# Three expert tiles by unsplit float32 products and five by gathers, and projection weights in 4 KB rows

## The chip, the core and the metric

The kernel runs on one core of a Trainium2 chip. A core has TensorE (PE, matrix products; its weight loads are PEld), VectorE (DVE), ScalarE (ACT), GpSimd (POOL, here the issuer of indirect DMAs) and SyncE (SP, here the issuer of the plain DMAs), and 16 DMA engines that all queues share. The metric is device time in microseconds, the median of several runs.

## The reference, cut to what matters

One decoder layer on 1024 tokens of 1024 channels, in float32. A combined projection feeds two groups of heads (stick-breaking attention and a gated linear recurrence), an output projection adds them to the stream, and then comes a layer of single-neuron experts:

```python
q = einsum('td,dhk->thk', xc, w_query)            # 8 heads, two halves of 128
s = einsum('thpk,hpnk->thpn', q, sub_keys)        # 128 keys for each half
top_s, top_i = top_k(s, 16)                       # 16 best of each half
best_s, best_pos = top_k(all 16 x 16 sums, 16)    # 16 best pairs of each head
idx = ...                                         # one of 128 * 128 experts
g = softmax(best_s)
u, v = expert_u[idx], expert_v[idx]               # 8 heads x 16 = 128 experts a token
act = gelu(einsum('td,thkd->thk', xc, u))
y = einsum('thk,thkd->td', g * act, v)
```

So each token takes 128 of 16384 experts, and an expert is one row of 1024 float32 in each of two tables of 64 MB.

## The kernel before

The 1024 tokens are 8 tiles of 128, worked on in five groups (tile 0; 1 and 2; 3 and 4; 5 and 6; tile 7). The stages of the groups (`norm_in`, `in_proj`, `rg_proj`, `rg_lru`, `attention`, `out_proj`, `queries`, `select`) are put out in the order of the string `ORDER`; the framework then lays each engine's instructions into one fixed sequence by a timeline that it simulates when the program is built, and what comes earlier in the program goes first where two could run. Each engine works off its sequence in order.

The experts are computed in two ways.

*Gathered tiles* (0, 1, 2 and 7): `gather_block` takes slots of 128 tokens x 1 expert. For a slot, GpSimd gathers 128 rows of table u (0.524 MB, line 652), VectorE multiplies them with the normalised tokens and sums (line 663), ScalarE and VectorE make the weight, GpSimd gathers 128 rows of v, and VectorE adds them, weighted, to y (line 678). A tile has 128 slots, so 256 gathers. The first `FREE` blocks of 8 slots have no condition; each later block, of one slot, has a ScalarE copy ahead (line 660) that reads a mark which the dense experts write, so that it does not start before its turn. The buffers are `UV` = 4 in the pool `gat` and, once the dense stage has begun, `UV2` more in `gat2`; slots go to the pools by turns.

*Dense tiles* (3, 4, 5 and 6): `gates` builds, for each tile, a matrix of gate weights over all 16384 experts and stores it in DRAM (`gd`, by a product `pg` for each token, line 623). `dense_experts` then goes over 128 blocks of 128 experts. For each, SP loads the block of the transposed u table (`ur`) and of the v table (`vr`), 0.524 MB each, and every fourth time a piece of the gate matrices (`gt`). Operands are split into two parts of type float32r, a high part by ScalarE and the remainder by VectorE (`split`, lines 182 and 183), and each product is three matmuls (`mm`, line 177): the scores `s` (8 chunks of channels x 3, 512 tokens wide), and the outputs, for four tiles and two halves of the channels. Six of these eight outputs stay in PSUM (`acc`); the other two go through a rotating bank (`rot`) every four blocks and are added in SBUF (`yr`).

The projection weights are read as tiles of 128 columns, from the matrix as it stands, so a row of a tile is 512 bytes in DRAM (`columns`, line 188); w_out is read in rows of 2 KB (line 426). Over the five groups these are 100 loads of w_in, 80 of w_q and 40 of w_out, each of 0.524 MB.

Of the kernel before, what the change touches and what calls it, by code (L numbers as in the profile page):

```python
# [7 lines left out]
F32 = mybir.dt.float32  # L8
F32R = mybir.dt.float32r
# [22 lines left out]
UV2 = 3  # L32
TB = 32
GE = 4
# [13 lines left out]
ORDER = "n0 i0 p0 a0 r0 o0 q001 q023 n1 i1 q047 s001 s047 p1 r1 a1 n2 p2 i2 o1 q1 r2 s023 n3 p3 i3 a2 r3 o2 q2 n4 s1 s2 i4 a3 p4 r4 o3 free g3 a4 q3 o4 s3 q4 g4 g5 g6 s4"  # L48
# [9 lines left out]
def layer(ctx, tc, x, w_in, w_out, w_q, vecs, rga, rgx, skT, eu, ev, euT, out,  # L58
          groups=((0,), (1, 2), (3, 4), (5, 6), (7,)), dense=(3, 4, 5, 6), dbg=None):
# [13 lines left out]
    # the banks that the last stages do not use are apart: the dense experts start in them  # L73
# [8 lines left out]
    # gate matrices of the dense tokens: gd[j, block of TB tokens, i, token], for expert i * 128 + j  # L82
# [36 lines left out]
    # means over 512 channels, over the channels of a head  # L119
# [6 lines left out]
    # heads 2 c and 2 c + 1 of 8 to chunk c of channels  # L126
# [14 lines left out]
    # rank16[k, s] = k  # L141
# [6 lines left out]
    # softplus(-lam) = max(-lam, 0) + ln(1 + exp(-|lam|))  # L148
# [18 lines left out]
    def cut(parts_, k, sl=slice(None)):  # L167
        return tuple(t[:, k, sl] for t in parts_)

    def mm(dst, a, b, first=True, last=True):  # L170
        """dst += sum over k of a[k].T @ b[k]: float32, or pairs of float32r parts"""
        n = len(a)
        terms = ((0, 0),) if len(a[0]) == 1 else ((1, 0), (0, 1), (0, 0))
        i = 0
        for u, v in terms:
            for k in range(n):
                nc.tensor.matmul(dst, a[k][u], b[k][v], start=first and i == 0, stop=last and i == len(terms) * n - 1)  # L177
                i += 1

    def split(hi, lo, src):  # L180
        """src as two float32r parts"""
        nc.scalar.activation(hi, src, AF.Copy)  # L182
        nc.vector.tensor_tensor(lo, src, hi.bitcast(F32), op=OP.subtract)  # L183

    def columns(pool, tag, w, c0, name, bufs):
# [37 lines left out]
    # sums of pairs in rows of 8: what no pair takes stays out of reach  # L223
# [3 lines left out]
    # the sums and the normalised rows of the gathered tiles  # L227
# [3 lines left out]
    def norm_in(g):  # L231
# [7 lines left out]
        # x -> h^T  # L239
# [5 lines left out]
    def in_proj(g):  # L245
# [6 lines left out]
        # q, k, v; q stays without its rstd, which the scores take  # L252
        rqk = keep.tile([P, 3, n, 8], F32, tag="rq", name="rq", bufs=2)
        G[g]["rq"] = rqk[:, 1:3]
        for dst, c1, gain, nm in ((kT[:, :, t0:t0 + T], 4, 1, "pk"), (qT, 0, 0, "pq")):
            for c in range(4):
                raw = columns(pj, "wraw", w_in, (c1 + c) * P, "wi", WI)
# [22 lines left out]
        for c in range(4):  # L280
            raw = columns(pj, "wraw", w_in, 1024 + c * P, "wi", WI)
# [6 lines left out]
    def rg_proj(g):  # L288
        """channels on partitions"""
# [4 lines left out]
        for e in range(4):  # L294
            wx = columns(pj, "wraw", w_in, 1536 + e * P, "wx", WI)
# [547 lines left out]
```

## Time and profile before

| | us |
|---|---|
| median of 3 runs | 2895.28 |
| lowest, highest | 2887.94, 2907.56 |
| span of the profiled execution, first to last instruction | 2904.6 |
| TensorE matmul busy | 2659.0 (92%) |
| VectorE busy | 2404.2 (83%) |
| GpSimd busy | 1401.6 (48%) |
| ScalarE busy | 1336.3 (46%) |
| 16 DMA engines, mean | 306 GB/s, 888.90 MB |

The span is the only time that the page has of the profiled execution itself. An engine's busy time is an average over stages with different limits, so the stages are looked at one by one: the projections and heads until about 1490 us, with gathers running beside them, and from there the dense experts, with paced gathers beside them.

### The profile page before, as it was taken

The numbers are of one execution on the slowest core, as the hardware profiler recorded it, in microseconds if no ns is written. First come the engines' busy times: TensorE is split into PE (matmuls) and PEld (weight loads), VectorE is DVE, ScalarE is ACT, GpSimd is POOL, SyncE is SP. The second block draws the span as 40 slices with busy tenths as digits, with TensorE's granted clock in tenths as the row PEclk, the third lists the DMA queues.
The fourth block names the chain that finished last, engine by engine and source line by source line (L and its number), as shares of the span: only waits on it lengthen the run. The fifth ranks groups of instructions, "written<-read, shape, count | busy, mean of one in ns | idle before, by whom it ended". The sixth has DMA issues, their size and how long they took to land.

```text
span 2904.6 us, 38604 instructions
## 1 busy us (share of the span) xinstructions
PE 2659.0 (92%) x12664; PEld 2103.5 (72%) x12664; DVE 2404.2 (83%) x5235; ACT 1336.3 (46%) x3255; POOL 1401.6 (48%) x1110
## 2 busy tenths in 40 slices
PE   7896989888997988988789999999999999999994
PEld 7685757766784576666567888888888888888883
DVE  2168779987998879998879979888888889888898
ACT  4426434434355633986834443434444434444432
POOL 0134654354444443323446546555655556555565
PEclk9997999898997889978889999999999999999997
DMA  8596888899977688987999989999999999999998
GB/s 235 162 325 223 289 308 297 268 308 297 293 237 250 226 288 291 327 285 268 334 321 360 347 315 365 328 338 352 323 347 339 333 325 352 334 348 329 335 331 307
DMA packets 470168, 888.90 MB, mean 306 GB/s; under 512 B 27600, under 2 KB 286672, under 8 KB 467920
## 3 DMA queue, kind: packets, MB, share of 16 engines
q0 software_dynamic: 147456, 536.94, 52.2%
q1 hardware_dynamic: 322512, 349.51, 36.1%
q8 instruction: 100, 1.64, 0.2%
q14 instruction: 100, 0.82, 0.1%
HBM read 841.25 MB, written 45.09 MB: 305 GB/s over the span
## 4 chain that ended last, share of the span: by engine, by line
PE 61%; DMA 13%; DVE 11%; issue 6%; ACT 5%; POOL 3%; SPq 0%; POOLq 0%; DVEq 0%; ACTq 0%
PE s L177 23%; PE acc L177 16%; PE rot L177 5%; DMA v<-in_ev_dram,idx 4%; DMA u<-in_eu_dram,idx 3%; DMA wq<-in_w_q_dram 3%; PE pqq L194 2%; PE pg L623 2%; DVE u L663 2%; PE pxg L194 2%; DVE y L678 2%; PE pv L285 2%; PE po L429 1%; PE z L377 1%; POOL v L652 1%
## 5 line engine op out<-in xcount | busy, mean ns | idle before, releaser
L652 POOL DMA_INDIRECT u<-in_eu_dram,idx x512 | 666.7, 1302 | 702.0 <-DVE y L678 340.5
L652 POOL DMA_INDIRECT v<-in_ev_dram,idx x512 | 665.2, 1299 | 609.7 <-DVE y L678 193.0
L678 DVE SCALAR_TENSOR_TENSOR y<-v,dots,y 128x1024 f32<-128x1024 f32 x512 | 654.9, 1279 | 48.4 <-DMA v<-in_ev_dram,idx 43.4
L663 DVE SCALAR_TENSOR_TENSOR u<-u,h 128x1024 f32<-128x1024 f32 x512 | 617.3, 1218 | 63.3 <-DMA u<-in_eu_dram,idx 62.0
L177 PE MATMUL s<-h2T,uh 128*128 128x512 f32 x2048 | 505.2, 396 | 0.0
L177 PEld LDWEIGHTS s<-h2T,uh 128*128 128x128 f32 x2048 | 385.5, 188 | 93.4 <-issue 0.2
L177 PE MATMUL acc<-vh,wl 128*128 128x512 f32 x768 | 300.1, 391 | 21.3 <-DVE wl L183 21.2
L177 PE MATMUL acc<-vl,wh 128*128 128x512 f32 x768 | 300.5, 391 | 0.1
L177 PE MATMUL acc<-vh,wh 128*128 128x512 f32 x768 | 299.9, 391 | 0.0
L177 PE MATMUL s<-h2T,ul 128*128 128x512 f32 x1024 | 264.3, 398 | 2.0 <-DVE ul L183 2.0
L194 PE MATMUL pqq<-act,wq 128*128 128x256 f32 (+1 forms) x1280 | 243.1, 347 | 10.9 <-DMA wq<-in_w_q_dram 10.9
L194 PEld LDWEIGHTS pqq<-act,wq 128*128 128x128 f32 x1280 | 208.7, 196 | 36.1 <-DMA wq<-in_w_q_dram 13.1
L177 PEld LDWEIGHTS s<-h2T,ul 128*128 128x128 f32 x1024 | 193.2, 189 | 49.3 <-DVE ul L183 1.8
L182 ACT ACTIVATE vh<-vr 128x512 fp32r<-128x512 f32 x256 | 159.1, 627 | 149.1 <-PE acc L177 70.1
L183 DVE TENSOR_TENSOR vl<-vr,vh 128x512 fp32r<-128x512 f32 x256 | 174.4, 687 | 50.6 <-ACT vh L182 47.1
L623 PE MATMUL pg<-oa,ob 128*128 128x128 f32 x1024 | 166.1, 315 | 37.8 <-DVE ob L620 26.6
L623 PEld LDWEIGHTS pg<-oa,ob 128*128 128x128 f32 x1024 | 148.2, 221 | 64.4 <-issue 22.4
L177 PEld LDWEIGHTS acc<-vh,wl 128*128 128x128 f32 x768 | 144.8, 189 | 53.6 <-issue 21.0
L717 ACT ACTIVATE ga<-s 128x512 f32<-128x512 f32 x128 | 76.4, 597 | 222.9 <-PE s L177 221.3
L624 ACT ACTIVATE gs<-pg 128x512 f32<-128x512 f32 x128 | 136.2, 1080 | 86.2 <-PE pg L623 69.4
L183 DVE TENSOR_TENSOR ul<-ur,uh 128x1024 fp32r<-128x1024 f32 x128 | 156.4, 1222 | 14.3 <-ACT uh L182 13.5
L177 PEld LDWEIGHTS acc<-vl,wh 128*128 128x128 f32 x768 | 144.9, 189 | 31.8 <-DVE vl L183 0.5
(238 smaller groups left out, 4445.1 us busy)
## 6 DMA issues: line engine op xcount, KB each, us to landing
vr<-in_ev_dram SPq DMA_DIRECT2D x128, 512.0 KB
ur<-in_euT_dram SPq DMA_DIRECT2D x128, 512.0 KB
wq<-in_w_q_dram SPq DMA_DIRECT2D x80, 512.0 KB
gd<-gs SPq DMA_DIRECT2D x16, 2048.0 KB
gt<-gd SPq DMA_DIRECT2D x32, 1024.0 KB
wi<-in_w_in_dram SPq DMA_DIRECT2D x60, 512.0 KB
wo<-in_w_out_dram SPq DMA_DIRECT2D x40, 512.0 KB
wx<-in_w_in_dram SPq DMA_DIRECT2D x20, 512.0 KB
```

Source lines behind the costliest of these rows:

```text
L177: nc.tensor.matmul(dst, a[k][u], b[k][v], start=first and i == 0, stop=last and i == len(terms) * n - 1)
L182: nc.scalar.activation(hi, src, AF.Copy)
L183: nc.vector.tensor_tensor(lo, src, hi.bitcast(F32), op=OP.subtract)
L194: nc.tensor.matmul(dst, w[:, k, :], act[:, k, :], start=k == 0, stop=k == DK - 1)
L285: nc.tensor.matmul(pv[:, i * P:(i + 1) * P], act[:, k, i * P:(i + 1) * P], raw[:, k, :], start=k == 0, stop=k == DK - 1)
L377: nc.tensor.matmul(zz, qT[pp, h // 2, qs], kT[pp, h // 2, c0:c0 + w], start=True, stop=not diag)
L623: nc.tensor.matmul(pg[:, t * P:(t + 1) * P], ob[:, t, :], oa[:, t, :], start=True, stop=True)
L624: nc.scalar.activation(gs[:, :, t4:t4 + 4].rearrange("p i t -> p t i"), pg.rearrange("p (t i) -> p t i", t=4), AF.Copy)
L652: nc.gpsimd.indirect_dma_start(out=t, out_offset=None, in_=table, in_offset=bass.IndirectOffsetOnAxis(ap=idx[:, s:s + 1], axis=0))
L663: nc.vector.scalar_tensor_tensor(u, u, 1.0, h2, op0=OP.mult, op1=OP.mult, accum_out=dots[:, s:s + 1])
L678: nc.vector.scalar_tensor_tensor(y, v, dots[:, s:s + 1], y, op0=OP.mult, op1=OP.add)
L717: nc.scalar.activation(ga, sp[:, :ND], AF.Gelu_apprx_tanh)
```

## The change

Tile 6 moves from the dense experts to the gathered ones: three tiles (384 tokens) are dense, five gathered. The dense products are no longer split: a matmul of float32 operands takes the place of three of float32r ones, and all six outputs (three tiles, two halves) stay in PSUM, so that `split`, `mm`, the rotating bank and the sums in SBUF go. The first 37 blocks of gathers (296 slots) have no condition (27 before, 216 slots). The pool of gathers in the dense stage has 12 buffers in place of 3, `ur` 4 in place of 3, `vr` 4 in place of 2, and a piece of the gate matrices covers 8 blocks of experts in place of 4, so its rows are 1 KB in place of 512 bytes. w_in, w_q and w_out are laid out on the host so that each partition's share of a tile is one row of 4 KB; the keys `skT` are laid out by head. The gates of tile 6 (`g6`) leave `ORDER`. Comments go.

```diff
-UV2 = 3
+UV2 = 12
-GE = 4
+GE = 8
-FREE = 27
-V0 = 2
-V1 = 5
-UR = 3
-VR = 2
+FREE = 37
+UR = 4
+VR = 4
-ORDER = "... g3 a4 q3 o4 s3 q4 g4 g5 g6 s4"
+ORDER = "... g3 a4 q3 o4 s3 q4 g4 g5 s4"
...
-          groups=((0,), (1, 2), (3, 4), (5, 6), (7,)), dense=(3, 4, 5, 6), dbg=None):
+          groups=((0,), (1, 2), (3, 4), (5, 6), (7,)), dense=(3, 4, 5), dbg=None):
...
-        nc.sync.dma_start(raw, w[:, c0:c0 + P].rearrange("(k p) n -> p k n", p=P))
+        nc.sync.dma_start(raw, w[c])
...
-                nc.sync.dma_start(raw, w_out[q * 256:(q + 1) * 256, c * 512:(c + 1) * 512].rearrange("(k p) n -> p k n", p=P))
+                nc.sync.dma_start(raw, w_out[c, q])
...
-            nc.sync.dma_start(skh, skT[:, 2 * h:2 * h + 2, :])
+            nc.sync.dma_start(skh, skT[h])
...
     def dense_experts():
-        act = [d1.tile([P, DK, ND], F32R, name=f"h2T{i}") for i in range(2)]
+        h2T = d1.tile([P, DK, ND], F32, name="h2T")
         for t, tl in enumerate(dense):
-            r = d1.tile([P, DK, P], F32, tag="ur", name="h2r", bufs=UR)
-            nc.sync.dma_start(r, h2Td[tl])
-            split(*(a[:, :, t * P:(t + 1) * P] for a in act), r)
...
-        quads = [(t, d) for d in range(2) for t in range(nt)]
-        held, rot = quads[:6], quads[6:]
+            nc.sync.dma_start(h2T[:, :, t * P:(t + 1) * P], h2Td[tl])
+        quads = [(t, d) for t in range(nt) for d in range(2)]
+        acc = {q: pd.tile([P, 512], F32, name=f"acc{q[0]}_{q[1]}") for q in quads}
...
         def front(e):
             ur = d1.tile([P, DK, P], F32, tag="ur", name="ur", bufs=UR)
             nc.sync.dma_start(ur, euT[e])
-            uh = d0.tile([P, DK, P], F32R, tag="uh", name="uh", bufs=2)
-            ul = d0.tile([P, DK, P], F32R, tag="ul", name="ul", bufs=2)
-            split(uh, ul, ur)
-            vr = d0.tile([P, D], F32, tag="vr", name="vr", bufs=VR)
-            nc.sync.dma_start(vr, ev[e * P:(e + 1) * P, :])
+            vs[e] = d0.tile([P, D], F32, tag="vr", name="vr", bufs=VR)
+            nc.sync.dma_start(vs[e], ev[e * P:(e + 1) * P, :])
             sp = pd0.tile([P, 512], F32, tag="s", name="s", bufs=2)
-            mm(sp[:, :ND], [cut((uh, ul), k) for k in range(DK)], hk)
-            ga = d1.tile([P, ND], F32, tag="ga", name="ga", bufs=2)
+            for k in range(DK):
+                nc.tensor.matmul(sp[:, :ND], ur[:, k, :], h2T[:, k, :], start=k == 0, stop=k == DK - 1)
+            ga = d1.tile([P, ND], F32, tag="ga", name="ga", bufs=3)
             nc.scalar.activation(ga, sp[:, :ND], AF.Gelu_apprx_tanh)
             gb = ga.rearrange("p (b t) -> p b t", t=TB)
             nc.vector.tensor_tensor(gb, gb, gts[0][:, :, e % GE, :], op=OP.mult)
-            wh = dp.tile([P, ND], F32R, tag="wh", name="wh", bufs=GE + 1)
-            wl = dp.tile([P, ND], F32R, tag="wl", name="wl", bufs=GE + 1)
-            split(wh, wl, ga)
-            wts[e] = (wh, wl)
+            wts[e] = ga
...
         def back(e):
-            for q in held:
-                vprod(acc[q], e, q, e == 0, e == P - 1)
-            if e % GE == GE - 1:
-                for q in rot:
-                    pr = pd0.tile([P, 512], F32, tag="s", name="rot", bufs=2)
-                    for f in range(e - GE + 1, e + 1):
-                        vprod(pr, f, q, f == e - GE + 1, f == e)
...
+            for t, d in quads:
+                nc.tensor.matmul(acc[t, d], wts[e][:, t * P:(t + 1) * P], vs[e][:, d * 512:(d + 1) * 512], start=e == 0, stop=e == P - 1)
...
+    def columns(w):
+        return w.reshape(DK, P, -1, P).transpose(2, 1, 0, 3)
...
+        "x": a["x"][0], "w_in": columns(a["w_in"][0]), "w_q": columns(a["peer_w_query"][0].reshape(D, 2048)),
+        "w_out": a["w_out"][0].reshape(4, 2, P, 2, 512).transpose(3, 0, 2, 1, 4),
```

## Rows read from the trace of the kernel before

**Rows 1.** The page: busy engines; DMA queues (packets, MB, share of time).
```profile
PE 2659.0 (92%) x12664; PEld 2103.5 (72%) x12664; DVE 2404.2 (83%) x5235; ACT 1336.3 (46%) x3255; POOL 1401.6 (48%) x1110
...
q0 software_dynamic: 147456, 536.94, 52.2%
q1 hardware_dynamic: 322512, 349.51, 36.1%
```

**Rows 2.** Windows by stage; engines busy (instructions), clock, DMA share, GB/s.
```profile
0.00:250.00 250.00, 195.12 (x1242) 172.29 (x1242) 100.13 (x413) 109.08 (x264) 49.56 (x59) 0.91 0.76 234
250.00:600.00 350.00, 318.13 (x1533) 245.10 (x1534) 304.46 (x844) 150.95 (x354) 175.48 (x150) 0.92 0.86 288
600.00:1000.00 400.00, 357.95 (x1795) 265.12 (x1794) 348.48 (x942) 196.69 (x436) 189.85 (x158) 0.88 0.82 266
1000.00:1490.00 490.00, 415.41 (x2151) 303.25 (x2150) 421.67 (x1169) 316.21 (x656) 168.22 (x151) 0.86 0.87 301
1490.00:2836.00 1346.00, 1344.60 (x5830) 1095.65 (x5829) 1174.12 (x1783) 551.60 (x1503) 778.36 (x563) 1.00 0.94 338
```

**Rows 3.** Windows, dense stage: the highest DMA share over 50 and over 20 us.
```profile
1750.00:1800.00 50.00, 50.00 (x218) 40.72 (x218) 44.86 (x70) 21.62 (x60) 30.46 (x23) 1.00 0.99 365
...
2500.00:2520.00 20.00, 20.00 (x89) 16.35 (x88) 15.99 (x25) 6.53 (x18) 9.44 (x8) 1.00 1.04 395
```

**Rows 4.** Waits, 1490 to 2836 us: total, times, longest.
```profile
POOL u L652 <- DVE y L678: 267.4, 111, 14.8
...
ACT dots L660 <- DVE y L678: 184.4, 136, 3.1
```

**Rows 5.** Groups by line: two VectorE splits (count, busy us, mean ns).
```profile
L183 DVE TENSOR_TENSOR vl<-vr,vh 128x512 fp32r<-128x512 f32 x256 | 174.4, 687 | 50.6 <-ACT vh L182 47.1 <-DMA vr<-in_ev_dram 2.0 <-issue 0.2
...
L183 DVE TENSOR_TENSOR ul<-ur,uh 128x1024 fp32r<-128x1024 f32 x128 | 156.4, 1222 | 14.3 <-ACT uh L182 13.5 <-issue 0.4
```

**Rows 6.** Groups by line, VectorE, 250 to 1490 us.
```profile
L678 DVE SCALAR_TENSOR_TENSOR y<-v,dots,y 128x1024 f32<-128x1024 f32 x201 | 256.5, 1276 | 34.5 <-DMA v<-in_ev_dram,idx 33.2
L663 DVE SCALAR_TENSOR_TENSOR u<-u,h 128x1024 f32<-128x1024 f32 x201 | 242.9, 1216 | 46.6 <-DMA u<-in_eu_dram,idx 46.3
L620 DVE SCALAR_TENSOR_TENSOR ob<-d,tr 128x512 f32<-128x512 f32 x128 | 86.9, 682 | 14.2 <-PE d L603 13.3 <-issue 0.7
...
L611 DVE TENSOR_TENSOR oa<-tr,iof 128x512 f32<-128x512 f32 x48 | 32.7, 686 | 10.3 <-PE pg L623 9.7 <-ACT tr L586 0.4
...
L663 DVE DVE_READ_ACCUMULATOR u<-u,h 128x1 f32 x201 | 16.3, 81 | 0.0
```

**Rows 7.** Windows of line 652 alone: gathers issued by 250 us.
```profile
0.00:250.00 250.00, 30.85 (x28) 0.91 0.76 234
```

**Rows 8.** Chain (start, us, what) and timeline: TensorE rows at full clock.
```profile
570.18 7.12 PE L194 MATMUL pxg<-act,wx 128*128 128x256 f32 x32
...
1614.06 5.62 PE s L177 x24
...
1691.15 4.12 PE acc L177 x18
...
1668.04 5.44 PE rot L177 x24
```

**Rows 9.** Timeline of TensorE: gate products, two of one tile.
```profile
1399.86 1.16 PE L623 MATMUL pg<-oa,ob 128*128 128x128 f32 x8
...
1440.54 1.16 PE L623 MATMUL pg<-oa,ob 128*128 128x128 f32 x8
```

**Rows 10.** Windows: weights alone on the DMA engines.
```profile
100.00:125.00 25.00, 24.07 (x104) 17.62 (x103) 2.23 (x6) 7.34 (x22) 4.00 (x4) 1.00 0.65 190
125.00:150.00 25.00, 24.56 (x175) 22.57 (x174) 8.23 (x59) 7.64 (x19) 3.21 (x2) 1.00 0.67 188
```

**Rows 11.** Chain by line: 0 to 250, then 250 to 1490 us.
```profile
by line: DMA wq<-in_w_q_dram 11.6%; PE pxg L194 10.8%; PE pv L285 8.9%; PE pq L194 8.2%; PE pqq L194 7.8%; issue 6.3%; PE pk L194 5.6%; PE po L429 4.4%; DMA wo<-in_w_out_dram 4.4%; DMA wi<-in_w_in_dram 3.6%; SPq L188 2.1%; ACT L322 1.5%; PE
...
by line: issue 10.8%; DMA v<-in_ev_dram,idx 7.5%; DMA u<-in_eu_dram,idx 5.8%; PE pg L623 5.2%; DVE u L663 4.4%; DVE y L678 4.1%; PE pqq L194 4.1%; DMA wq<-in_w_q_dram 3.6%; PE pxg L194 2.8%; PE z L377 2.3%; DVE ti L479 2.2%; ACT gs L624 2.1
```

More of the change, by code (lines that the diff above doesn't have):

```diff
@@ L38 @@
 GS = 1
[L40 to L44 removed]
+FREE = 37
+UR = 4
+VR = 4
 WI = 4
 WO = 3
[L48 removed]
+ORDER = "n0 i0 p0 a0 r0 o0 q001 q023 n1 i1 q047 s001 s047 p1 r1 a1 n2 p2 i2 o1 q1 r2 s023 n3 p3 i3 a2 r3 o2 q2 n4 s1 s2 i4 a3 p4 r4 o3 free g3 a4 q3 o4 s3 q4 g4 g5 s4"
 NB = 8
@@ L165, in layer, with columns @@
     nc.vector.memset(hs_tail, 0.0)
[L167 to L185, printed above, removed]
+    def columns(pool, tag, w, c, name, bufs):
         raw = pool.tile([P, DK, P], F32, tag=tag, name=name, bufs=bufs)
-        nc.sync.dma_start(raw, w[:, c0:c0 + P].rearrange("(k p) n -> p k n", p=P))
+        nc.sync.dma_start(raw, w[c])
         return raw
@@ L256, in in_proj @@
             for c in range(4):
-                raw = columns(pj, "wraw", w_in, (c1 + c) * P, "wi", WI)
+                raw = columns(pj, "wraw", w_in, c1 + c, "wi", WI)
                 pq = b_in(nm)
@@ L280, in in_proj @@
         for c in range(4):
-            raw = columns(pj, "wraw", w_in, 1024 + c * P, "wi", WI)
+            raw = columns(pj, "wraw", w_in, 8 + c, "wi", WI)
             pv = b_in("pv")
@@ L294, in rg_proj @@
         for e in range(4):
-            wx = columns(pj, "wraw", w_in, 1536 + e * P, "wx", WI)
-            wg = columns(pj, "wraw", w_in, 2048 + e * P, "wg", WI)
+            wx = columns(pj, "wraw", w_in, 12 + e, "wx", WI)
+            wg = columns(pj, "wraw", w_in, 16 + e, "wg", WI)
             pxg = b_in("pxg")
@@ L460, in queries @@
             for s in range(2):
-                raw = columns(wk, "wo", w_q, (2 * h + s) * P, "wq", WO)
+                raw = columns(wk, "wo", w_q, 2 * h + s, "wq", WO)
                 chans_mm(pq[:, s * 256:s * 256 + T], raw, act)
@@ L683, in dense_experts @@
         nt = len(dense)
-        act = [d1.tile([P, DK, ND], F32R, name=f"h2T{i}") for i in range(2)]
+        h2T = d1.tile([P, DK, ND], F32, name="h2T")
         for t, tl in enumerate(dense):
-            r = d1.tile([P, DK, P], F32, tag="ur", name="h2r", bufs=UR)
-            nc.sync.dma_start(r, h2Td[tl])
-            split(*(a[:, :, t * P:(t + 1) * P] for a in act), r)
-        hk = [cut(act, k) for k in range(DK)]
-        quads = [(t, d) for d in range(2) for t in range(nt)]
-        held, rot = quads[:6], quads[6:]
-        acc = {q: pd.tile([P, 512], F32, name=f"acc{q[0]}_{q[1]}") for q in held}
-        yr = {q: dp.tile([P, 512], F32, name=f"yr{q[0]}_{q[1]}") for q in rot}
-        wts, vs = {}, {}
-        def vprod(dst, e, q, first, last):
-            t, d = q
-            mm(dst, [tuple(w[:, t * P:(t + 1) * P] for w in wts[e])], [vs[e][d]], first=first, last=last)
-        gts = {}
+            nc.sync.dma_start(h2T[:, :, t * P:(t + 1) * P], h2Td[tl])
+        quads = [(t, d) for t in range(nt) for d in range(2)]
+        acc = {q: pd.tile([P, 512], F32, name=f"acc{q[0]}_{q[1]}") for q in quads}
+        wts, vs, gts = {}, {}, {}
         def front(e):
             if e % GE == 0:
-                gts[0] = dp.tile([P, NBLK, GE, TB], F32, tag="gt", name="gt", bufs=2)
+                gts[0] = d1.tile([P, NBLK, GE, TB], F32, tag="gt", name="gt", bufs=2)
                 nc.sync.dma_start(gts[0], gd[:, :, e:e + GE, :])
@@ L719, in front @@
             nc.vector.tensor_tensor(gb, gb, gts[0][:, :, e % GE, :], op=OP.mult)
[L720 to L723 removed]
+            wts[e] = ga
             for k in range(n_turn):
                 if (k * P + PH) // n_turn == e:
[L726 to L748 removed]
+                    nc.scalar.activation(turn[:, k:k + 1], ga[:, 0:1], AF.Copy)
+        def back(e):
+            for t, d in quads:
+                nc.tensor.matmul(acc[t, d], wts[e][:, t * P:(t + 1) * P], vs[e][:, d * 512:(d + 1) * 512], start=e == 0, stop=e == P - 1)
         front(0)
@@ L755, in dense_experts @@
         for t, d in quads:
-            xo = d1.tile([P, 512], F32, tag="ga", name="xo", bufs=2)
+            xo = d1.tile([P, 512], F32, tag="xo", name="xo", bufs=2)
             tl = dense[t]
             nc.sync.dma_start(xo, x1d[tl][:, d * 512:(d + 1) * 512])
-            nc.vector.tensor_tensor(xo, xo, acc[t, d] if (t, d) in acc else yr[t, d], op=OP.add)
+            nc.vector.tensor_tensor(xo, xo, acc[t, d], op=OP.add)
             nc.sync.dma_start(out[tl * P:(tl + 1) * P, d * 512:(d + 1) * 512], xo)
```

17 lines of the change are left out of this document (1 added, 16 removed).

## Prediction

> **What bounds the kernel now.** Four views were read, in this order. The page first: TensorE is busy 92% of the span, VectorE 83%, and the two DMA queues hold the 16 DMA engines 52.2% and 36.1% of it, together 88.3% [rows 1]. Three resources are near their limit, and the page doesn't say which one ends each stage. The windows by stage do [rows 2]. In the dense stage, 1490 to 2836 us, TensorE is busy throughout at a granted clock of 1.00 (the 2.4 GHz level), VectorE is at 87%, and the DMA engines at 0.94. TensorE sets that stage: the waits say that GpSimd and the paced copies wait for VectorE's sums [rows 4], which in turn come when a mark lets them, so the gathers follow TensorE's pace and the DMA share is what that pace asks for. The reader is to see how little is left: 0.94 on average, 0.99 in the best 50 us and 1.04 in the best 20 us (two packets can overlap at one engine) [rows 3]. Before 1490 us nothing is full. VectorE is at 87% (1074.6 of 1240 us), the DMA engines at 0.82 to 0.87, TensorE at 85 to 91% with the clock at 0.86 to 0.92, so at times on the 1.2 GHz level [rows 2]. There the chain runs through many engines, 13% of it through gathers on which VectorE, in order, stands still [rows 11].
>
> **The DMA ledger.** This is the sum that I rest on, in DMA time, i.e. busy time averaged over the 16 engines. Before: 0.883 x 2904.6 = 2565 us.
> One gather costs 0.522 x 2904.6 / 1024 = 1.48 us [rows 1]. Tile 6 brings 2 x 128 = 256 more: +379 us.
> The weights: 220 loads, 115.3 MB. While almost nothing but weights moves, in 512 byte rows for the most part, 190 and 188 GB/s go at a share of 0.65 and 0.67 [rows 10], so 286 GB/s at a full share; the dense stage, mostly 4 KB rows, has 338 at 0.944, so 358 [rows 2]. 115.3 MB take 403 us in short rows and 322 in long ones: -81. Bounds: 0, if row length isn't what differs between the two stretches, and -120, if weights alone came near the 395 GB/s of the best 20 us [rows 3].
> The gate pieces `gt`: 33.5 MB in 512 byte rows (117 us by the 286) become 25.2 MB in 1 KB rows, between 70 us (358) and 88 us (286); I take 79: -38. Gate stores `gd`: four of 16 go, 8.4 MB at 358: -23. The moves of tile 6's normalised rows change form, not amount: 0. So does `skT`, whose rows were 1 KB already.
> After: 2565 + 379 - 81 - 38 - 23 = 2802 us. That alone is 96% of the present span.
>
> The row length has a rule to be weighed. The trace shows 286 against 358 GB/s at a full share [rows 2, 10]. The Trainium skill, page "DMA: Bandwidth & Descriptors", section Specifications, gives 512 bytes as the least transfer for line rate; by it the weights' long rows would gain nothing, the ledger would end at 2883 us, and the sum below would be some 20 us higher, since the weights move where the DMA engines aren't full. The trace disagrees with it by a quarter.
>
> **TensorE, VectorE and ScalarE in the dense stage.** Before, a block of 128 experts takes 24 score matmuls in 5.62 us, 18 into `acc` in 4.12 and a quarter of 48 `rot` ones (24 in 5.44): 11.10 us [rows 8]. After: a float32 matmul goes as two instructions; 32 of them, 256 columns wide, take 7.12 us with the drain, about 218 ns each [rows 8]. By width 384 columns take 327 ns and 512 take 435. Eight score products are 16 x 0.327 = 5.23 us, six output products 12 x 0.435 = 5.22: 10.45 us, so 1338 us for 128 blocks against 1421. Three quarters of the tokens at four thirds of the passes would be no change; the 6% come from the smaller time per column.
> VectorE loses the splits: 1.22 us for `ul`, 0.69 twice for `vl` [rows 5], the same width again for `wl` and half of one for `yr`, 3.6 us a block or 465 us in all, and gains 48 slots of some 2.7 us. ScalarE loses the high parts. Neither sets the stage then, so both gains count for nothing by themselves: TensorE hides them now, and the DMA engines will.
> What is late next is the gathers. If all goes as `FREE` says, 344 slots are left for the stage, 688 gathers or 1019 us of DMA time; `ur` and `vr` are 134.2 MB, 375 us; `gt` 79, results and the like 20: 1493 us, against TensorE's 1338. The deeper buffers let GpSimd and SP run further ahead. They lift the share towards full, but make no bandwidth. SP's queue holds `ur`, `vr` and `gt`, GpSimd's the gathers, and both end in the same 16 engines.
>
> **How far the first stage gets.** It ends earlier. Gate products of one tile come every 1.77 us for 4 tokens (the two rows are 23 steps apart) [rows 9], 32 steps, 57 us, and they stand at the end of the stage, so `g6` going is worth 57 us (0 if select of tile 7 is what ends late). Weights are 20% of the chain before 250 us (11.6 + 4.4 + 3.6) and 3.6% after [rows 11], 49 + 45 us; a fifth less is -20 (0 to -60). 1490 - 57 - 20 = 1413.
> But VectorE must do 80 more slots in it. Of its 1074.6 us after 250, the 201 slots took 256.5 + 242.9 + 16.3 = 515.7 (2.57 each), the rest 559 [rows 6]. Without `g6` (a quarter of `ob`'s 86.9, a third of `oa`'s 32.7, together 33) and the first splits (24) 502 remain. From 250 to 1413 are 1163 us. At the present 87% that leaves 198 slots, at 100% 257; I take 90%, 212. With the 14 before 250 [rows 7] that is 226 slots, 452 gathers, where 592 were meant (the bounds are 424 and 542). So 140 gathers slide into the dense stage, whose VectorE has room, but whose DMA engines have none.
>
> **The sum.** From 1413 us on: 828 gathers x 1.48 = 1225, `ur` and `vr` 375, `gt` 79, the rest 20: 1699 us of DMA time. I take a share of 1.02, between the best 50 us and the best 20 us [rows 3], as for queues that are never empty: 1666 us. With 10 us for the last sums and the store: 1413 + 1666 + 10 = 3089 us of span. The page has no other time of that execution; its span lies 9 us above the median of the three runs, so 3080 us.
> Bounds: VectorE filled in the first stage (542 gathers) and a share of 1.04: 1565 / 1.04 = 1505, 2919. The share kept at 0.944, with 452 gathers done: 1800, 3214.
>
> **The rivals.** *The first stage takes its 592 gathers* (12 in 100). VectorE's sequence is laid out when the program is built, and 165 us of it stand idle, 80 of these in front of gathers that had not landed [rows 6], which leaner weights would bring sooner. Against it: with the idle time wholly filled only 542 fit. Then 1493 / 1.02 = 1464, and 1413 + 1464 + 10 - 9 = 2878 us, no change within 1%.
> *TensorE sets the dense stage* (6 in 100), the case in which the change is worth something: 1413 + 1338 + 15 - 9 = 2757 us. It needs 1493 us of DMA time in 1338, a share of 1.12, which no 20 us of the dense stage show.
> *The order of VectorE's work holds up TensorE* (10 in 100), slower than my forecast: a block's weights `ga` wait on VectorE behind a product whose rows haven't landed. Such waits took 80 us of the first stage [rows 6]; with late gathers in the dense stage TensorE stops, its clock falls and the loads of `ur` and `vr` stop with it. Then the share stays at 0.94: 3205 us. It decides once three blocks of `ga` no longer bridge a late gather.
> *The DMA engines set the end*, as summed (72 in 100): slower, 2919 to 3200.
>
> **How the numbers follow.** A measurement of this kernel tells 1%, 29 us, from no change. Faster by more has the TensorE case and a little of the first rival: 0.08. Within 1% is the rest of that rival: 0.10. Slower: 0.82. The range goes from 2910 (the lower bound of the sum) to 3190; it leaves out the TensorE case, most of the first rival and half of the order case, 2 in 10.
>
> **What would show it.** In the changed profile: matmuls of `s` at 327 ns spacing and of `acc` at 435; no splits; a DMA share of 0.98 or more for over 1500 us, with GpSimd waiting for buffers and VectorE for rows; TensorE done with the dense experts well ahead of the end, or pausing in them; about 450 gathers issued by the start of the dense blocks; 512 byte rows gone and weights at 350 GB/s. I am wrong if a 4 KB packet costs less once the short rows are gone (the ledger's 1.48), or if VectorE packs its slots into the first stage.

## The result, and the profile after

The changed kernel takes 3172.47 us (median of 4 runs, 3161.32 to 3182.41) against 2898.28 (4 runs, 2887.94 to 2907.56): a ratio of 1.0934, interval 1.0886 to 1.0982, so 274 us slower. The profiled execution has a span of 3159.1 us.

The page of the changed kernel: busy engines, TensorE's and the DMA engines' slices (79 us each), the two queues, as in [rows 1].

```profile
PE 2485.4 (79%) x9790; PEld 1579.1 (50%) x9790; DVE 2287.4 (72%) x5080; ACT 934.5 (30%) x2726; POOL 1614.1 (51%) x1366
...
PE   7979798989978989659999999999999999300000
...
DMA  6587887898677888779999999999899999999997
...
q0 software_dynamic: 184320, 671.17, 58.3%
q1 hardware_dynamic: 115824, 332.73, 28.6%
```

TensorE went from 92% of the span to 79%, and not by being slower: its digits are 9 from slice 19 to slice 34, and then it has nothing more to do while the DMA engines work on. The queues held the engines 0.869 x 3159.1 = 2745 us, against 2565 before.

The windows of the changed kernel by stage, the columns of [rows 2] (its first stage ends at 1395 us, its dense blocks at 2715):

```profile
0.00:250.00 250.00, 204.37 (x1289) 180.35 (x1290) 110.90 (x437) 112.85 (x272) 51.81 (x64) 0.91 0.67 240
250.00:600.00 350.00, 312.46 (x1501) 241.17 (x1500) 297.00 (x824) 147.89 (x347) 172.82 (x147) 0.91 0.81 285
600.00:1000.00 400.00, 360.71 (x1874) 263.85 (x1873) 358.57 (x955) 207.83 (x460) 193.56 (x162) 0.92 0.79 276
1000.00:1395.00 395.00, 298.52 (x1590) 219.45 (x1589) 316.25 (x1018) 223.30 (x472) 141.46 (x126) 0.84 0.84 306
1395.00:2715.00 1320.00, 1309.37 (x3543) 674.26 (x3541) 836.84 (x1276) 185.22 (x893) 718.25 (x598) 1.00 0.95 354
2715.00:3159.00 444.00, 0.00 (x0) 0.00 (x0) 367.87 (x574) 57.38 (x283) 336.26 (x272) 0.50 0.92 334
```

The last row is where the time went. For 444 us TensorE stands idle, its granted clock down at 0.50, while 272 gathers come in one after another. The row above it, the dense stage, has TensorE busy for 1309 of 1320 us at 1.00; VectorE has fallen to 63% (836.8 of 1320), and the DMA engines are at 0.95, hardly above the 0.94 of before, although GpSimd now had 12 extra buffers. The first stage ended earlier and the rest took longer, together 254 us of span. The bounds of the two sets of windows, 1490 and 1395, aren't the same event. The first `acc` matmul is, here before and after:

```profile
1463.92 0.76 PE L177 MATMUL acc<-vh,wl 128*128 128x512 f32 x1 [20.83 <-DVE wl L183]
```
```profile
1394.13 5.31 PE L695 MATMUL acc<-vr,ga 128*128 128x512 f32 x12
```

By it the first stage is 70 us shorter, and what follows 324 us longer (1765 against 1441).

The same windows by the line of the gathers, for the stretch after 1395 us:

```profile
1395.00:1800.00 405.00, 193.17 (x167) 1.00 0.91 333
1800.00:2715.00 915.00, 525.08 (x431) 1.00 0.96 363
2715.00:3159.00 444.00, 336.26 (x272) 0.50 0.92 334
```

So 1280 - 167 - 431 - 272 = 410 gathers were issued before 1395. Left alone at the end, one takes 444 / 272 = 1.63 us.

The waits of the changed kernel, 1395 to 2715 us (total, times, longest):

```profile
DVE ga L686 <- ACT ga L684: 252.9, 83, 9.8
...
POOL v L632 <- DVE y L658: 207.1, 92, 40.6
...
POOL u L632 <- DVE u L643: 165.8, 62, 9.3
DVE u L643 <- DMA u<-in_eu_dram,idx: 94.9, 73, 4.3
DVE y L658 <- DMA v<-in_ev_dram,idx: 85.0, 60, 4.0
```

This is the row that I had not foreseen. VectorE, which is to empty the gather buffers, stands for 253 us in front of `ga`, the gate product of a dense block whose scores TensorE has not finished. It works in its fixed sequence, and GpSimd waits behind it for buffers. The rows for its next slots have mostly landed: after 69 of the 72 such waits of more than 0.5 us VectorE's next instruction started at once. How many slots the sequence places beside the dense blocks can be counted, by the sums into y (line 658) that VectorE has done before the last `ga` product (2703 us):

```profile
0.00:2703.00 2703.00, 631.97 (x493) 0.94 0.86 316
```

So 493 of 640 slots stand ahead of the last `ga` and 147 behind it. The tail of gathers was laid out when the program was built; it doesn't come of transfers that were late in this execution. Nor did late gathers hold up TensorE in the dense stage, as it was busy for 1309 of 1320 us. The longest wait for `ga` lies at the hand-over between the stages, here in the timeline of the changed kernel (start, us, what; in brackets the idle time before and what ended it):

```profile
1378.53 15.76 PE L682 MATMUL s<-h2T,ur 128*128 128x384 f32 x40 [52.42 <-DMA ur<-in_euT_dram]
...
1388.49 0.56 DVE L686 TENSOR_TENSOR ga<-ga,gt 128x384 f32<-128x384 f32 x1 [39.65 <-ACT ga L684]
...
1499.80 5.32 PE L682 MATMUL s<-h2T,ur 128*128 128x384 f32 x16
1504.96 5.31 PE L695 MATMUL acc<-vr,ga 128*128 128x512 f32 x12
1510.11 5.33 PE L682 MATMUL s<-h2T,ur 128*128 128x384 f32 x16
```

The first `ur` took until 1378 us, and VectorE stood 40 us at the first `ga`. The last three rows are one dense block at speed: 16 score instructions in 5.16 us (322 ns each), 12 output ones in 5.15 (429 ns).

### The profile page after: what moved, and what is told of

Its sections match the earlier page's. It is cut to its first block, busy times and chain, and to the rows that moved or that the text cites. A ratio compares the mean times of both kernels' runs of the same rounds, so it can differ in the third digit from the quotient of the medians.

```text
span 3159.1 us, 32684 instructions
## 1 busy us (share of the span) xinstructions
PE 2485.4 (79%) x9790; PEld 1579.1 (50%) x9790; DVE 2287.4 (72%) x5080; ACT 934.5 (30%) x2726; POOL 1614.1 (51%) x1366
## 4 chain that ended last, share of the span: by engine, by line
PE 42%; DMA 20%; issue 13%; DVE 12%; POOL 8%; ACT 6%; SPq 0%; POOLq 0%; DVEq 0%; ACTq 0%
PE s L682 15%; PE acc L695 15%; DMA v<-in_ev_dram,idx 9%; DMA u<-in_eu_dram,idx 9%; POOL u L632 4%; POOL v L632 3%; DVE u L643 3%; PE pxg L174 3%; DVE y L658 2%; PE pqq L174 2%; PE pv L265 1%; PE pk L174 1%; ACT oa L588 1%; DMA ur<-in_euT_dram 1%; PE z L357 1%
## 5 line engine op out<-in xcount | busy, mean ns | idle before, releaser
L632 POOL DMA_INDIRECT v<-in_ev_dram,idx x640 | 790.7, 1235 | 728.2 <-DVE y L658 307.1
L632 POOL DMA_INDIRECT u<-in_eu_dram,idx x640 | 755.6, 1181 | 640.3 <-DVE u L643 237.3
L658 DVE SCALAR_TENSOR_TENSOR y<-v,dots,y 128x1024 f32<-128x1024 f32 x640 | 821.0, 1283 | 151.6 <-DMA v<-in_ev_dram,idx 136.7
L643 DVE SCALAR_TENSOR_TENSOR u<-u,h 128x1024 f32<-128x1024 f32 x640 | 776.9, 1220 | 196.8 <-DMA u<-in_eu_dram,idx 195.8
L682 PE MATMUL s<-h2T,ur 128*128 128x384 f32 x2048 | 684.0, 488 | 52.4 <-DMA ur<-in_euT_dram 52.4
L695 PE MATMUL acc<-vr,ga 128*128 128x512 f32 x1536 | 682.3, 594 | 8.4 <-DVE ga L686 8.4
L682 PEld LDWEIGHTS s<-h2T,ur 128*128 128x128 f32 x2048 | 391.1, 191 | 351.1 <-issue 114.9
L695 PEld LDWEIGHTS acc<-vr,ga 128*128 128x128 f32 x1536 | 292.5, 191 | 351.2 <-issue 307.2
L409 PE MATMUL po<-wo,act 128*128 128x512 f32 x256 | 125.9, 640 | 7.2 <-DMA wo<-in_w_out_dram 5.3
L357 PE MATMUL z<-kT,qT 64*128 64x128 f32 (+3 forms) x192 | 94.9, 588 | 6.1 <-ACT om L363 5.8
```

The lines of the kernel that those rows point to most:

```text
L357: nc.tensor.matmul(zz, qT[pp, h // 2, qs], kT[pp, h // 2, c0:c0 + w], start=True, stop=not diag)
L409: nc.tensor.matmul(acc[i], act[:, 2 * q + k, i * P:(i + 1) * P], raw[:, k, :], start=q == 0 and k == 0, stop=q == 3 and k == 1)
L632: nc.gpsimd.indirect_dma_start(out=t, out_offset=None, in_=table, in_offset=bass.IndirectOffsetOnAxis(ap=idx[:, s:s + 1], axis=0))
L643: nc.vector.scalar_tensor_tensor(u, u, 1.0, h2, op0=OP.mult, op1=OP.mult, accum_out=dots[:, s:s + 1])
L658: nc.vector.scalar_tensor_tensor(y, v, dots[:, s:s + 1], y, op0=OP.mult, op1=OP.add)
L682: nc.tensor.matmul(sp[:, :ND], ur[:, k, :], h2T[:, k, :], start=k == 0, stop=k == DK - 1)
```

## The experiments

Two accounts stood against each other. In D the DMA engines set the pace of the gathers, and the time is DMA work divided by what they can move. In O VectorE's fixed sequence sets it: the engines have room that the order doesn't use. A third, N, has the number of gathers set the pace, not their bytes.

### The parts of the change by themselves

**Long weight rows alone**, in the kernel before.

```diff
-nc.sync.dma_start(raw, w[:, c0:c0 + P].rearrange("(k p) n -> p k n", p=P))
+nc.sync.dma_start(raw, w[c])
...
+    def columns(w):
+        return w.reshape(DK, P, -1, P).transpose(2, 1, 0, 3)
```

> The kernel before with the 4 KB rows of w_in, w_q and w_out alone; four tiles stay dense and split. Three accounts stand against each other over this set of runs. Account D: the 16 DMA engines set the pace of the gathers, in the dense stage and after it. Account O: VectorE's fixed sequence sets how many gathers go beside each dense block, and what it leaves over runs alone at the end. Account N: the number of gather instructions on GpSimd and VectorE sets it. All three give this run the same: the weights' DMA time falls by some 80 us (403 to 322), of which 20 us (0 to 60) are on the path of the first stage, and the dense stage stays TensorE's at 11.1 us a block. 2878 us (2840 to 2900). If row length bought nothing, 2898.

Measured: 2893.27 us (12 runs), ratio 0.997 (0.9937 to 1.0004): no difference that can be told. Its queue row, its windows where weights move nearly alone and in the dense stage, and its first `acc` matmul:

```profile
q1 hardware_dynamic: 156112, 349.51, 33.5%
```
```profile
100.00:125.00 25.00, 24.69 (x111) 18.30 (x110) 1.38 (x2) 8.81 (x25) 4.00 (x4) 1.00 0.57 179
125.00:150.00 25.00, 25.00 (x189) 23.48 (x189) 11.49 (x82) 6.40 (x17) 3.21 (x2) 1.00 0.61 201
...
1490.00:2836.00 1346.00, 1344.78 (x5832) 1095.98 (x5831) 1173.41 (x1786) 551.55 (x1502) 775.32 (x561) 1.00 0.94 338
```
```profile
1471.90 0.77 PE L177 MATMUL acc<-vh,wl 128*128 128x512 f32 x1 [20.51 <-DVE wl L183]
```

Packets of q1 fell from 322512 to 156112 and its DMA time from 1049 us [rows 1] to 0.335 x 2912.6 = 976, with the same bytes: 73 us of DMA time saved, and no time that can be told (the interval allows 18 us). At a full share weights now move at 179 / 0.57 = 314 and 201 / 0.61 = 330 GB/s, 286 before [rows 10]. The dense stage is as busy as it was [rows 2], and in this execution, 8 us longer than that of the kernel before, it began 8 us later. The first stage has DMA room, with shares of 0.76 to 0.87 before, so that what is saved there was hardly anyone's wait.

**Unsplit products alone**, four dense tiles kept.

```diff
-            split(uh, ul, ur)
...
-            mm(sp[:, :ND], [cut((uh, ul), k) for k in range(DK)], hk)
+            mm(sp[:, :ND], [cut((ur,), k) for k in range(DK)], hk)
...
-            split(wh, wl, ga)
-            wts[e] = (wh, wl)
+            wts[e] = (ga,)
```

> The kernel before (four dense tiles, four gathered, old rows) with unsplit float32 products alone. By the float32 rows 16 + 16 instructions of 512 columns at 0.435 us are 13.9 us a block against 11.1, 1782 us against 1421: 2898 + 361 = 3260 (3220 to 3290), TensorE at 100% and the DMA share falling to some 0.76 in the dense stage. If VectorE's splits were what paced the dense stage, under 2900.

Measured: 3214.96 us, ratio 1.1077 (1.0917 to 1.1237), just under the range that I gave. A window of its dense stage:

```profile
2000.00:2200.00 200.00, 200.00 (x467) 88.54 (x466) 98.57 (x155) 28.68 (x126) 77.20 (x65) 1.00 0.75 262
```

TensorE is full, at 200 / 467 = 428 ns an instruction, 32 of them or 13.7 us a block against 11.10 before [rows 8], and the DMA engines are down at 0.75 (0.80 from 1600 to 2400 us). So unsplit products on four tiles make TensorE the limit by a wide margin. For three tiles they take 10.31 us a block, less than the split ones for four (11.10), but more than the split ones for three (8.1 in the next run).

**Three dense tiles, products still split**, long rows, `FREE` 37, buffers as before.

```diff
-FREE = 27
+FREE = 37
...
-dense=(3, 4, 5, 6)
+dense=(3, 4, 5)
```

> Three dense tiles and five gathered, as in the changed kernel, with the long weight rows and FREE = 37, but with the split products and the buffers of the kernel before. What the move of one tile costs, apart from the products. D: the DMA ledger is that of the changed kernel but for gt (512 byte rows, +10 us), so the time is too: 3150 to 3220, with TensorE done early (8.3 us a block, 1066 us of dense work). If the unsplit products made the loss: near the kernel before or faster, 2750 to 2950. N: 3100 to 3300, since VectorE then has 400 us of splits on top of 1280 gathers' products.

Measured: 3288.28 us, ratio 1.133 (1.122 to 1.144), some 70 us beyond what I expected of it. Its windows, dense stage and after:

```profile
1400.00:2440.00 1040.00, 1037.78 (x5250) 943.33 (x5249) 880.02 (x1326) 443.67 (x1164) 492.20 (x376) 1.00 0.94 338
2440.00:3280.00 840.00, 5.54 (x25) 4.26 (x23) 637.68 (x1008) 101.40 (x500) 661.90 (x498) 0.51 0.91 317
```

TensorE is through in 1040 us (8.1 a block), with only 376 gathers beside it; 498 then come alone, at 840 / 498 = 1.69 us each. A dense stage that is faster than the gathers gives nothing back, and here it loses: the gathers that it leaves over run alone, at a share of 0.91. The changed kernel, with slower unsplit products that end nearer to the gathers, is better by 4 points, about one of them by the deeper buffers (below). VectorE's splits are also gone there, and no run divides the rest.

### DMA work or VectorE's order

**Half the dense loads.** `ur` and `vr` are loaded for every second block and used for two.

```diff
-            ur = d1.tile([P, DK, P], F32, tag="ur", name="ur", bufs=UR)
-            nc.sync.dma_start(ur, euT[e])
+            if e % 2 == 0:
+                us[e] = d1.tile([P, DK, P], F32, tag="ur", name="ur", bufs=UR)
+                nc.sync.dma_start(us[e], euT[e])
...
+            else:
+                us[e], vs[e] = us[e - 1], vs[e - 1]
```

> The changed kernel, in which ur and vr are loaded for every second block of experts only and used twice (half the experts' products are left out of the dense result). 128 loads of 0.524 MB go, 67 MB, 188 us of DMA time; no instruction of TensorE, VectorE or GpSimd goes. D: the gathers take the time that comes free, 3172 - 188 = 2985 us (2960 to 3020), and fewer gathers are left when TensorE is done (some 150 in place of 272). O and N: the same number of gathers beside the dense blocks and the same 444 us after them, 3130 to 3180.

Measured: 3011.01 us, ratio 1.0374 (1.0304 to 1.0444), 161 us less than the change. Its windows:

```profile
1800.00:2760.00 960.00, 954.38 (x2588) 492.17 (x2587) 731.86 (x1164) 174.14 (x866) 670.99 (x536) 1.00 0.95 358
2760.00:3014.00 254.00, 1.31 (x4) 0.24 (x2) 217.73 (x340) 33.26 (x164) 189.99 (x155) 0.51 0.92 336
```

**Half the bytes of a gather.** Each gather fetches rows of 512 elements, which VectorE uses twice, at its full width.

```diff
-            t = pool.tile([P, D], F32, tag="uv", ...)
+            t = pool.tile([P, 512], F32, tag="uv", ...)
-            nc.gpsimd.indirect_dma_start(out=t, in_=table, ...)
+            nc.gpsimd.indirect_dma_start(out=t, in_=table.rearrange("n (h d) -> (n h) d", d=512), ...)
```

> The changed kernel with gathers of half a row, 2 KB (each half is used twice, so the experts of the gathered tiles are wrong in half of their channels). As many gathers, as many and as wide products on VectorE, half the bytes: 336 MB less, some 900 us of DMA time. D: the DMA engines are then far from full, TensorE's dense stage sets the end: 1395 + 1320 + 15, 2700 to 2790 us, gathers done with it. N: 1280 gathers and 1280 products as before, 3100 to 3180. O: between, 2950 to 3150, with a tail of over 100 gathers after TensorE.

Measured: 2813.33 us, ratio 0.9693 (0.9628 to 0.9758). A window of its dense stage:

```profile
1600.00:2400.00 800.00, 720.14 (x1879) 359.84 (x1878) 682.48 (x1100) 147.01 (x731) 615.36 (x522) 0.97 0.84 280
```

Both take DMA work away and give time back, 161 us of the 188 that D expects in the one, 359 in the other. In the second no gather is left after the dense blocks, the DMA share falls to 0.84, and VectorE (85%), TensorE (90%) and GpSimd (615 us, and 0.30 us ahead of each of 522 gathers: 772 of 800) are the next limits, a little above D's figure. The 3100 us and more that N expects are out for the whole kernel. But between D and O these two runs don't decide: other transfers also change the timeline from which VectorE's sequence is laid out. The sums into y ahead of the last `ga`, with half the loads and with half the bytes of a gather:

```profile
0.00:2754.80 2754.80, 710.17 (x554) 0.94 0.86 309
```
```profile
0.00:2792.20 2792.20, 818.90 (x638) 0.94 0.72 239
```

554 and 638 slots stand there, where the changed kernel has 493. So both runs had another sequence with a shorter tail, and O can claim their gain as well as D.

**The gathers emitted in their turn**, each block ahead of the dense block after which it is due; nothing else.

```diff
+        def turns(e):
+            for k in range(n_turn):
+                if (k * P + PH) // n_turn == e:
+                    gather_block(*next(coming))
...
                 front(e + 1)
+                turns(e + 1)
```

> The changed kernel with the blocks of gathers put into the program in their turn: the 37 free blocks ahead of the dense experts, each later block right behind the dense block that marks its turn, so that they stand ahead of the next dense block's work in the fixed sequences (in the changed kernel all stand behind the dense experts). Same work. O: VectorE no longer stands at a dense block's ga while rows lie ready, the gathers keep up, the end is TensorE's or VectorE's: 2750 to 2900. D: the DMA time left after the first stage is 1650 us and can't be less: 1395 + 1650 = 3045 (3030 to 3110), TensorE pausing for gathers in place of the tail.

Measured: 3174.44 us, ratio 1.0948 (1.0888 to 1.1007): as the change, which is neither account's figure. The wait of VectorE in its dense stage, and the sums into y ahead of the last `ga`, show why:

```profile
DVE ga L686 <- ACT ga L684: 296.3, 84, 38.6
```
```profile
0.00:2717.20 2717.20, 631.73 (x493) 0.94 0.87 314
```

VectorE still stands at `ga`, and as many slots stand ahead of each of the 128 `ga` products as in the changed kernel (493 ahead of the last). The order in the program alone didn't move them, so the edit didn't do what O needed, and the run tells nothing of D against O.

**Gathers with nothing beside them.** 8 of the 128 dense blocks are computed, so nearly all paced gathers run alone; once with full rows, once with half rows.

```diff
+NE = 8
...
-        for e in range(P):
-            if e + 1 < P:
+        for e in range(NE):
+            if e + 1 < NE:
```

> The changed kernel with 8 of 128 dense blocks (120 are left out, so the dense tiles' result is not the layer's), so that nearly 800 gathers run with nothing beside them. To be read against the next run, which differs in the bytes of a gather alone. D: 1.50 us a gather at a DMA share of 0.95, about 2690 us in all. If a gather by itself is held by VectorE (1.33 us of work for each) or by the chain from buffer to gather to product, the share is under 0.9 and the next run has the same time.

> As the run before it, with gathers of half a row (2 KB; the gathered experts use each half twice). D: the DMA engines are at 0.6 and VectorE sets the pace, 1.35 to 1.40 us a gather against 1.50, 80 to 120 us faster than the run before it. If VectorE or the chain held the full rows too, within 30 us of it.

Measured, one run each: 2859.53 us and 2656.5. The windows with full rows (the second by the line of the gathers alone), and with half rows:

```profile
1600.00:1800.00 200.00, 0.00 (x0) 0.00 (x0) 135.52 (x182) 3.81 (x19) 124.27 (x105) 0.50 0.84 280
...
1800.00:2600.00 800.00, 629.93 (x513) 0.50 0.94 340
```
```profile
1800.00:2600.00 800.00, 628.88 (x554) 0.50 0.65 185
...
2000.00:2200.00 200.00, 0.00 (x0) 0.00 (x0) 172.53 (x277) 28.14 (x139) 157.94 (x139) 0.50 0.64 181
```

The largest waits of GpSimd with half rows, in the same 800 us (total, times, longest; "issue" is time in which it waited for nothing that the profile shows):

```profile
POOL u L633 <- issue: 78.0, 256, 0.3
POOL v L633 <- issue: 59.1, 194, 0.3
```

Full rows take 800 / 513 = 1.56 us a gather at a share of 0.94, half rows 1.44. So the bytes count, but halving them brings only 8%. VectorE is then at 86% (172.5 of 200 us), and GpSimd has nothing left: 628.88 us of gather instructions and 0.30 us ahead of each make 795 of the 800 us, and with full rows 784. So for gathers alone N isn't out. GpSimd issues them one behind the other in both runs, and a gather instruction took 1.23 us with full rows and 1.14 with half, 0.93 at the least; what draws it out isn't shown (spans on GpSimd are rough). Gathers alone have limits close together.

Both runs missed. The first is 170 us above its forecast, and the blocks without a mark make some 100 of it: from 1395 to 1800 us 201 gathers were issued in 405 us, where 1.50 each are 302. They use 4 buffers, and a gather takes 200 / 105 = 1.9 us there at a share of 0.84. Such a block also has 8 slots in place of 1, and no run divides the two. The second is 203 us faster than the first, where I had 80 to 120.

**Dense blocks kept to the gathers.** In the order of the run with the gathers in their turn, the gelu of every fourth dense block takes as its bias a zero that VectorE makes behind the gathers due by then. TensorE can't run ahead, and the sequence is laid out accordingly.

```diff
+        for e in need.get(order.index((n, b, nb)), ()):
+            nc.vector.tensor_scalar(hold[:, e // 4:e // 4 + 1], y[:, 0:1], 0.0, None, op0=OP.mult)
...
-            nc.scalar.activation(ga, sp[:, :ND], AF.Gelu_apprx_tanh)
+            nc.scalar.activation(ga, sp[:, :ND], AF.Gelu_apprx_tanh, bias=hold[:, e // 4:e // 4 + 1])
```

> The kernel of run e6 (gathers in their turn) with the dense experts held to the pace of the gathers: every fourth block's gelu reads, as its bias, a zero made from y behind the gather that should be done by then (214 of 640 slots at the first block, the rest in even steps), so no tail can be left. It tells the DMA engines from VectorE's sequence: if gathers fall behind only by where they stand in that sequence, holding the dense blocks costs little and the tail of 440 us goes, 2750 to 2950. If the DMA engines are the limit, TensorE pauses by as much as the tail was long, share 0.94 to 0.96 throughout: 1395 + 1662 / 0.95 = 3145 (3110 to 3200).

Measured: 3058.97 us, ratio 1.0547 (1.0489 to 1.0605): 113 us back with the same transfers, between the two accounts. Its windows and VectorE's wait:

```profile
1395.00:1800.00 405.00, 277.67 (x717) 141.16 (x716) 246.66 (x351) 30.70 (x126) 211.75 (x181) 0.84 0.90 318
1800.00:3000.00 1200.00, 1073.97 (x2820) 548.69 (x2819) 909.67 (x1445) 218.31 (x1024) 803.97 (x660) 0.95 1.01 392
```
```profile
DVE ga L697 <- ACT ga L695: 71.6, 42, 11.0
```

TensorE is now made to pause (its clock is 0.95), and yet the kernel is faster: VectorE stands at `ga` for 72 us in place of 253, no gathers are left to run alone, and the DMA engines hold 1.01 and 392 GB/s for 1200 us. So D alone is wrong, as the engines had 6% more than they gave. The sequence is another: 623 slots now stand ahead of the last `ga`. The stretch to 1800 us, where the unmarked blocks with 4 buffers still run, stays at 0.90.

**Buffers, and fewer unmarked blocks**, each alone on the change.

```diff
-UV2 = 12
+UV2 = 3
```

> The changed kernel with 3 buffers in place of 12 in the second pool of gathers. Run e2 had 3, and its gathers alone at the end went at a share of 0.90, 1.66 us each, against 0.93 and 1.59 in run e7 with 12. Full DMA engines need enough gathers in flight: 272 x 0.07 = 20 us in the tail and some 20 in the dense stage, 3210 (3180 to 3240). If depth does nothing, 3172, and the 116 us by which e2 is slower than the changed kernel are from VectorE's splits alone.

```diff
-FREE = 37
+FREE = 27
```

> The changed kernel with FREE back at 27 blocks (216 slots). 205 slots are done when the dense stage begins, so with 37 some 90 slots without a mark are left, which may use only the 4 buffers of the first pool; they run until 1800 us at a share of 0.92 (0.84 in run e7, with nothing beside them). With 27 all of the later ones have 16 buffers. By the DMA account the share goes to 0.95 there: -15 us, 3157 (3140 to 3175). If the marks hold gathers back, 3180 or more.

Measured: 3194.87 us, ratio 1.1022 (1.0974 to 1.107), with 3 extra buffers; 3151.4, ratio 1.0859 (1.0811 to 1.0907), with 27 unmarked blocks. The tail of the first and the start of the dense stage of the second:

```profile
2715.00:3186.00 471.00, 0.00 (x0) 0.00 (x0) 352.23 (x554) 55.36 (x273) 349.55 (x271) 0.50 0.89 311
```
```profile
1395.00:1800.00 405.00, 405.00 (x1102) 209.19 (x1101) 248.47 (x385) 64.71 (x322) 214.06 (x178) 1.00 0.92 350
```

The deeper buffers of the change were worth 22 us, as its tail is 27 us shorter (444 us against 471 for nearly the same gathers). Meaning more gathers for the first stage cost 21 us, as I had expected, but not by the reason that I gave: with 27 the share to 1800 us is 0.92 in place of 0.91, the gathers before and after 2715 us are as many as in the changed kernel (271 after it, 272), and the two profiled executions differ by 6 us only. Where the other 15 us lie isn't shown.

**Both: kept to the gathers, 27 unmarked blocks.**

```diff
-FREE = 37
+FREE = 27
```

> Run e10 (dense experts held to the gathers' pace) with FREE = 27, as in run e12. In e10 the share was 0.90 from 1395 to 1800 us, where blocks without a mark have 4 buffers, and 1.01 from 1800 to 3000, at 392 GB/s. If the 4 buffers made the low share and the DMA engines are the limit behind them, it goes to about 1.0 from the start: 1662 us of DMA time, 1395 + 1662 + 10 = 3067 less the gain by overlap, 3025 (3005 to 3050). If not, 3059 as e10. Either way not below 2990: the DMA work doesn't fit into the time of the kernel before.

Measured: 2996.23 us, ratio 1.0302 (1.0239 to 1.0365). It is below the range that I gave (3005 to 3050). Its windows, VectorE's wait, 1395 to 2930 us, and the sums into y ahead of the last `ga`:

```profile
1395.00:1800.00 405.00, 318.83 (x833) 163.21 (x832) 293.06 (x464) 68.11 (x326) 264.79 (x215) 0.89 0.98 375
1800.00:2930.00 1130.00, 1025.78 (x2694) 524.80 (x2693) 857.81 (x1369) 213.23 (x1038) 759.01 (x625) 0.95 1.01 396
```
```profile
DVE ga L697 <- ACT ga L695: 81.2, 44, 11.0
```
```profile
0.00:2939.10 2939.10, 798.70 (x623) 0.91 0.90 337
```

The two edits together give back 176 us (3172.47 to 2996.23), more than their sum of 134. DMA engines are at 0.98 and 1.01 from the end of the first stage on, and the kernel is still 3% slower than before. No version here that computes the layer beats the kernel before; the one with long rows is level with it.

## Why the prediction held, and where it didn't

**Direction and cause.** The direction and the time came as forecast, the cause in part. "That alone is 96% of the present span" is the step that held: the DMA work rose from 2565 to 2745 us, and with the order mended until the DMA engines are at 0.98 to 1.01 for 1535 us, 3.0% of slowdown remains, about a third of the 9.3%. That this third is work for which the DMA engines have no room is argued from that share; no run took bytes out of the best version. The other two thirds are how the gathers were placed, which the best version gets back without a byte less. My account, in which full DMA engines set the end, doesn't hold for them: the changed kernel ended late because VectorE's sequence had left 147 slots for after the dense blocks. Of the signs that I listed, a share of 0.98 for over 1500 us did not come. That the sum of a wrong share and a right ledger fell 70 us from the measured span is luck in part.

**The ledger.** 2802 forecast, 2745 measured. The weights' -81 came as -73. The gathers were the difference: 0.583 x 3159.1 / 1280 = 1.44 us each, not 1.48, which is some 50 us over all. I had named that as a way to be wrong; it is small.

**The row length.** With long rows weights move at 314 to 330 GB/s at a full share, against 286 [rows 10]: 10 to 15% more, not the quarter that I wrote. The changed kernel has the same, here by its windows of the weights alone:

```profile
100.00:125.00 25.00, 23.97 (x108) 17.79 (x108) 1.39 (x2) 8.45 (x25) 4.00 (x4) 1.00 0.57 185
125.00:150.00 25.00, 25.00 (x192) 23.57 (x191) 12.06 (x84) 6.65 (x18) 3.21 (x2) 1.00 0.62 197
```

So 512 byte rows were not yet at the full rate here, and the rule of the Trainium skill (page "DMA: Bandwidth & Descriptors", section Specifications) is contradicted in kind, by less than I claimed. My -20 us for it on the path of the first stage is not borne out: by themselves the rows were worth nothing that 12 runs can tell, and 18 us at the most by the interval.

**TensorE.** 327, 435 ns and 10.45 us a block were forecast; 322, 429 and 10.31 came, and 1320 us for the stage where I had 1338. That the splits' going from VectorE is worth nothing by itself, as I argued, no run tests alone.

**The first stage.** It ended at 1395, forecast 1413. My 1490 for the kernel before was 26 us behind its first `acc` matmul; from 1464 the same -77 would have given 1387. I can't divide the 70 us: no run took `g6` away alone. Gathers done by then: 410 against my 452, below even my lower bound of 424. I took VectorE at 90% of the time after 250 us; it was at (297.00 + 358.57 + 316.25) / 1145 = 85%, and the 40 us at the first `ga` count in that. So the rival of 592 gathers is out.

**The step that failed: "a share of 1.02, as for queues that are never empty".** After 1395 us there were 0.95 x 1320 + 0.92 x 444 = 1662 us of DMA time (1699 forecast) and they took 1764 us, a share of 0.942. At 1.02 they would have taken 1629, and with my 10 us for the last sums 1639: this term was 125 us too small, and the errors in the ledger and in the first stage hid a part of it (3089 forecast, 3159.1 measured). The size wasn't beyond the engines, as 1.01 in the two versions kept to the gathers shows. The share fell short in two places. In the dense stage VectorE's sequence had few slots beside each block, so that buffers came free late and GpSimd stood 373 us in its two largest waits for them; behind it the gathers ran alone, at 0.92.

**The rival nearest to it** had the right place and the wrong victim. I wrote that VectorE's order would hold up TensorE behind a late gather, with a share that stays at 0.94. The share did. But TensorE was busy for 1309 of 1320 us and its clock stayed at 1.00; it was the gathers that were held up behind a dense block's `ga`, for 253 us. TensorE ran off with its blocks, and the tail of gathers alone, at 0.92, is the rest of the price. (Its 3205 us are 9 too few: the same share gives 3214 in my bounds.) The rival in which TensorE sets the dense stage had the stage right, as TensorE was busy throughout, and the end wrong: 444 us of gathers were left behind it, and its 2757 us are out.

**What stays open.** That the sequence put the tail where it was is counted. That the stand at `ga` lowered the share rests on edits that also slowed TensorE down; no run freed VectorE of it with TensorE at full speed. By what rule the simulated timeline gives each dense block so few slots isn't on record. Nor did a run deepen both pools: single slots take the pools by turns, so that every second one still had 4 buffers, whatever `UV2` is. Why gathers alone stop at 0.94 with VectorE at some 80% isn't settled either. GpSimd, which issues them without a break, is the nearest candidate: in the tail of the changed kernel its 272 gathers fill 336 + 272 x 0.30 = 418 of 444 us.

## What to carry to other kernels

Before moving work from an engine to the DMA engines, add up DMA time per queue as a ledger: where it comes near the span, a saving on another engine buys nothing. That sum is a floor and not a forecast: here a share near 1 was reached only in the versions where the slow stream, the gathers, set the pace of the fast one, and an engine that finished early left the others to run alone at a lower share. Where one engine serves two streams in a fixed order, count in the trace what stands ahead of the last piece of the faster stream: what stands behind it runs alone, whatever the transfers do.

## What the runs showed of the hardware

Gathers and plain loads together held the 16 DMA engines at 1.01 for over 1100 us and 392 to 396 GB/s, where the best 20 us of the kernel before had 395 [rows 3]; gathers alone stopped at 0.94 and 340 GB/s (in the tail of the changed kernel 0.92 and 334) with 16 buffers in all, at 0.89 and 311 with 7, and at 0.84 and 280 with 4, there in blocks of 8 slots. With next to nothing to wait for, GpSimd issued a gather of 128 rows every 1.56 us with rows of 4 KB and every 1.44 us with rows of 2 KB. The DMA time of one gather isn't a constant of its size: by the page of each run 1.48 us before, 1.44 after, 1.49 with gathers mostly alone (0.669 x 2857.3 / 1280) and 1.40 in the best version (0.597 x 2992.7 / 1280).
